# Gate and residual of the MLP moved to the third step from the end in every block, the gated sum by way of PSUM

## The chip, the cores and the metric

The kernel runs on one core of a Trainium2 chip. The core has a matrix engine (TensorE, "PE" in the profile), VectorE ("DVE"), ScalarE ("ACT"), GpSimd ("POOL"), and SyncE ("SP"), which here only issues the transfers. They run their own instruction queues in order and wait for each other by semaphores. The metric is the device time of one execution in microseconds (us), smaller is better.

## The reference, cut to what matters

One layer of a diffusion backbone over 2048 tokens of width 1024: attention and convolution, and then the MLP that the change is about. All in fp32.

```python
x_new = x + g1 * (concat([attn_x, conv_x]) @ w_out)
hx2 = modulate(rms_norm(x_new, norm2_g), sh2, sc2)
x_new = x_new + g2 * (square(relu(hx2 @ w_mlp1)) @ w_mlp2)   # w_mlp1 (1024, 4096), w_mlp2 (4096, 1024)
return rms_norm(x_new, final_g)
```

`g2` is the gate, one value for each of the 1024 columns; the first `x_new` on the last line but one is the residual.

## The kernel before

Every product is made of three matmuls on halves of the numbers (`mm3`, lines 89 to 92: high by high, high by low, low by high). So each weight that arrives from memory is split into a high part (a ScalarE copy) and a low part (a subtraction on VectorE or GpSimd).

The MLP (lines 1374 to 1540) goes over 4 blocks of 512 tokens (`NBL`; a block is `TB` = 4 tiles of 128 tokens) and in each block over 16 steps (`NC`), one for each 256 of the 4096 hidden columns. A step `(b, c)` has two halves:

- `hidden` makes the hidden columns of the block by a Strassen-like scheme: seven products named `11`, `s2`, `s1`, `12`, `s3`, `22`, `s4` into PSUM, with VectorE sums between them (lines 1459 to 1471). Line 1459 reads the product `s2`; the product `22` is written over it, so TensorE can't begin `22` before line 1459 is done.
- `second` multiplies the hidden columns by the rows of `w_mlp2`, one 128x1024 product for each of the 4 tiles, and VectorE adds it to the tile's running sum `ac` (line 1497; a copy at `c == 0`, line 1490). It is issued one step late, after `hidden` of the next step.

`load_w1` and `load_w2` fetch the weights of the coming step into four buffers (`raw`) and split them: line 1392 on ScalarE, 1393 on GpSimd, the sums `s1` to `s4` of the weights on VectorE (line 1398), and for `w_mlp2` lines 1422 and 1423.

The gate and the residual go in once for each block, at step `CX[b]`, line 1374:

```python
    CX = [NC - 1] * (NBL - 1) + [NC - 3]
```

There VectorE multiplies `ac` by `g2` (line 1501) and GpSimd adds the residual `xf` (line 1502), which is loaded into one of the two `tmp` buffers (line 1500). In blocks 0 to 2 this is the last step, 15; in block 3 it is step 13. For steps after `CX[b]`, the rows of `w_mlp2` are multiplied by `g2` before they are split, on GpSimd (line 1420): two such instructions a step, so four in block 3. After step 15 a tile is squared on ScalarE (line 1505, into the `xf` buffer where that is still held, else into PSUM), scaled (line 1507) and stored.

At a block's end the tokens of the next one are transposed: `trans_next` loads them (`xm`, line 1430, into the same two `tmp` buffers), TensorE transposes them (line 1255), and ScalarE, VectorE and GpSimd make the split tiles `X` of them (lines 1260 to 1273; GpSimd's part is line 1269, tile `xtl`). These are issued at a high priority. The order of the instructions on each engine, and the buffer that each tile gets, are set when the kernel is built, by a scheduler that goes by its own estimates.

PSUM is one tile, `pall`, used as four slots of 128x1024 in rotation: two for `hidden`, one for each 128x1024 product of `second`, one for each transposed tile.

Of the kernel before, what the change touches and what calls it, by code (L numbers as in the profile page):

```python
# [14 lines left out]
ALU = mybir.AluOpType  # L15
# [26 lines left out]
def hybrid_layer(ctx: ExitStack, tc: tile.TileContext, a: dict, out: bass.AP):  # L42
    nc = tc.nc
    TE, VE, SE, GE, SY = nc.tensor, nc.vector, nc.scalar, nc.gpsimd, nc.sync
# [9 lines left out]
    def psA(name, hold=None):  # L54
        i = free_ps.popleft()
        (free_ps if hold is None else hold).append(i)
        return pall[:, i * 1024:(i + 1) * 1024]
# [31 lines left out]
    def mm3(outp, lh, ll, rh, rl, start, stop):  # L89
        TE.matmul(outp, lh, rh, start=start, stop=False)  # L90
        TE.matmul(outp, lh, rl, start=False, stop=False)  # L91
        TE.matmul(outp, ll, rh, start=False, stop=stop)  # L92
# [35 lines left out]
    def rstd_of(dst, ss, n=D):  # L128
        SE.activation(dst, ss, AF.Sqrt, bias=epst[0:dst.shape[0]], scale=1.0 / n)
        VE.reciprocal(dst, dst)  # L130
# [1147 lines left out]
    def tmp(name):  # L1278
        return mp.tile([P, D], F32, tag="tmp", bufs=2, name=name)

    def row(name):
        return mp.tile([P, D], F32, tag="row", bufs=3, name=name)

    def acc(name):
        return mp.tile([P, D], F32, tag="ac", bufs=TB, name=name)
# [66 lines left out]
    g2, fg, pu = row("g2"), row("fg"), row("pu")  # L1352
# [21 lines left out]
    NC = FF // 256  # L1374
    NBL = S // (TB * P)

    CX = [NC - 1] * (NBL - 1) + [NC - 3]


    def load_w1(c, nm):  # L1380
# [32 lines left out]
    def load_w2(b, c, nm):  # L1413
        t = ttile(f"w2_{nm}", ring)
        ws = []
        for kh in range(2):
            r = raw(f"w2_{nm}{kh}r")
            SY.dma_start(r, w2[c * 256 + kh * P:c * 256 + (kh + 1) * P, :])
            if c > CX[b]:
                GE.tensor_tensor(r, r, g2, ALU.mult)  # L1420
# [56 lines left out]
    def second(b, c, hid, w2s):  # L1477
        for tt in range(TB):
            t = b * TB + tt
            o = tt * P  # L1480
            po_ = psA(f"pm{b}_{c}_{tt}")
            for n in range(2):
                for fc in range(2):
                    hh, hl = hid[0][:, fc, :], hid[1][:, fc, :]
                    wh, wl = w2s[fc]
                    mm3(po_[:, n * 512:(n + 1) * 512], hh[:, o:o + P], hl[:, o:o + P],
                        wh[:, n * 512:(n + 1) * 512], wl[:, n * 512:(n + 1) * 512], fc == 0, fc == 1)
            if c == 0:
                accs[tt] = acc(f"ac{b}{tt}")
                VE.tensor_copy(accs[tt], po_)  # L1490
                continue
            ac = accs[tt]
            xt = po_
            if b == NBL - 1 and c == NC - 1 and tt == TB - 1:
                last_tile(t, po_, ac)
                return
            VE.tensor_tensor(ac, po_, ac, ALU.add)  # L1497
            if c == CX[b]:
                xt = tmp(f"xf{t}")
                SY.dma_start(xt, xn_d[t * P:(t + 1) * P, :])  # L1500
                VE.tensor_tensor(ac, ac, g2, ALU.mult)  # L1501
                GE.tensor_tensor(ac, xt, ac, ALU.add)
            if c == NC - 1:
                ss = mp.tile([P, 1], F32, tag="ssf", bufs=2, name=f"ssf{t}")
                SE.activation(xt, ac, AF.Square, accum_out=ss)
                rstd_of(ss, ss)
                VE.scalar_tensor_tensor(ac, ac, ss, fg, ALU.mult, ALU.mult)
                SY.dma_start(out[t * P:(t + 1) * P, :], ac)


    def last_tile(t, po_, ac):
        ss = mp.tile([P, 2], F32, tag="ssl", bufs=1, name="ssl")
        hs = [slice(n * 512, (n + 1) * 512) for n in range(2)]
        for n, h in enumerate(hs):
            VE.tensor_tensor(ac[:, h], po_[:, h], ac[:, h], ALU.add)
            SE.activation(po_[:, h], ac[:, h], AF.Square, accum_out=ss[:, n:n + 1])
        VE.tensor_tensor(ss[:, 0:1], ss[:, 0:1], ss[:, 1:2], ALU.add)
        rstd_of(ss[:, 0:1], ss[:, 0:1])
        for h in hs:
            VE.scalar_tensor_tensor(ac[:, h], ac[:, h], ss[:, 0:1], fg[:, h], ALU.mult, ALU.mult)  # L1520
            SY.dma_start(out[t * P:(t + 1) * P, h], ac[:, h])
# [3 lines left out]
    for i, (b, c) in enumerate(steps):  # L1525
        if c == 0 and pend_ is not None:
            second(*pend_)
            pend_ = None
        w2s = load_w2(b, c, f"{b}_{c}")
        hid = hidden(f"{b}_{c}", w1n)  # L1530
        if b == 0 and 2 <= c < KD + 5:
            g2_step(c - 2)
        if i + 1 < len(steps):
            if c == 0 and b:
                with tc.issue_after(lv):
                    w1n = load_w1((c + 1) % NC, "%d_%d" % steps[i + 1])
            else:
                w1n = load_w1((c + 1) % NC, "%d_%d" % steps[i + 1])
        if c == NC - 1 and b + 1 < NBL:
            X = new_X(b + 1)  # L1540
            n0 = len(nc.cur_bb.bb.instructions)
            for tt in range(TB):
                with tc.high_priority(offset=3000):
                    trans_next(b + 1, tt)

            lv = last_of(VE, n0)
        if pend_ is not None:
            second(*pend_)
        pend_ = (b, c, hid, w2s)
    second(*pend_)  # L1550


# [56 lines left out]
```

## Time and profile before

| | |
|---|---|
| median of 3 runs | 2568.53 us (2560.25 to 2570.44) |
| profiled execution, its own time | 2570.69 us |
| its span | 2568.9 us |
| mean granted TensorE clock | 0.979 |
| busy share of the span: PE, DVE, ACT, POOL | 95%, 70%, 49%, 57% |
| a block of the MLP (from step 2 of block 1 to step 2 of block 2) | 354.6 us |

The span is what the engines' first and last instructions enclose; the kernel's time lies 1.8 us above it. Busy shares are means over the whole kernel, in which the MLP is the second half, from about 1160 us on. In a view of one engine in order of time, a row has its start, its length, the line, the operation, what it writes and reads, and, in square brackets, how long the engine sat idle ahead of it and what it waited for.

### The profile page before, as it was taken

The page shows a single profiled execution, that of the slowest core. Times are in us where ns is not written, and L with a number is a line of the kernel's source. Part 1 is how long each engine was busy: PE and PEld are TensorE (multiplying, and loading weights), DVE is VectorE, ACT ScalarE, POOL GpSimd, SP SyncE. Part 2 cuts the span into 40 slices and gives each one's busy share as a digit, 9 for nine tenths or more (in the row PEclk, how much of TensorE's full clock was granted, in tenths as well). Part 3 has the DMA queues.
Part 4 walks back from the last instruction along what each step waited for, and adds up shares of the span by engine and source line. Part 5 has one row for each costly group of instructions (what it writes and reads, how often), then busy time and mean ns, then how long its engine had stood idle before and what let it go on. Part 6 is the DMA issues. An engine that isn't in the chain of part 4 may idle for free.

```text
span 2568.9 us, 42313 instructions
## 1 busy us (share of the span) xinstructions
PE 2430.5 (95%) x15903; PEld 2216.9 (86%) x15903; DVE 1790.2 (70%) x2465; ACT 1248.7 (49%) x2162; POOL 1467.8 (57%) x1055
## 2 busy tenths in 40 slices
PE   7997989899889999988999999999999999999997
PEld 5985889689889999987998889999889998799996
DVE  6646743666689976468666697666786676876676
ACT  4334531443689963134444554444554445454442
POOL 3537422442578856457555676555675556755564
PEclk9998999999999999999999999999999999999999
DMA  8555764653899865665333443333343334433321
GB/s 299 158 168 163 223 216 130 196 154 110 227 253 262 241 182 174 195 231 165 99 99 107 129 139 111 101 105 99 121 148 101 99 99 126 137 107 100 105 92 57
DMA packets 293882, 387.26 MB, mean 151 GB/s; under 512 B 38021, under 2 KB 231228, under 8 KB 293644
## 3 DMA queue, kind: packets, MB, share of 16 engines
q1 hardware_dynamic: 293660, 384.54, 49.7%
q8 instruction: 125, 2.05, 0.3%
q14 instruction: 81, 0.66, 0.1%
q10 hardware_dynamic: 16, 0.00, 0.0%
HBM read 308.03 MB, written 86.76 MB: 154 GB/s over the span
## 4 chain that ended last, share of the span: by engine, by line
PE 62%; DVE 10%; DMA 9%; POOL 5%; issue 4%; SPq 2%; ACT 1%; DVEq 0%; POOLq 0%; ACTq 0%
PE pall L90 18%; PE pall L91 18%; PE pall L92 18%; PE pall L1105 2%; PE pall L1069 1%; PE pall L1030 1%; DVE s L1398 1%; DMA ar<-at_d 1%; DVE ac L1501 1%; DVE ac L1497 1%; PE pall L1107 1%; DVE w L1423 1%; PE pall L1032 1%; DMA cw<-h_d 1%; DMA xn_d<-xo 1%
## 5 line engine op out<-in xcount | busy, mean ns | idle before, releaser
L90 PE MATMUL pall<-w,hh 128*128 128x512 f32 x1024 | 406.0, 397 | 11.0 <-DVE ac L1497 7.2
L91 PE MATMUL pall<-w,hh 128*128 128x512 f32 x1024 | 403.0, 394 | 0.0
L92 PE MATMUL pall<-w,hl 128*128 128x512 f32 x1024 | 397.2, 392 | 0.6 <-DVE hl L1454 0.6
L1497 DVE TENSOR_TENSOR ac<-pall,ac 128x1024 f32<-128x1024 f32 x239 | 286.8, 1214 | 73.9 <-PE pall L92 73.2
L90 PEld LDWEIGHTS pall<-w,hh 128*128 128x128 f32 x1024 | 195.1, 190 | 51.6 <-issue 4.4
L92 PEld LDWEIGHTS pall<-w,hl 128*128 128x128 f32 x1024 | 193.3, 189 | 41.9 <-DVE hl L1454 2.2
L91 PEld LDWEIGHTS pall<-w,hh 128*128 128x128 f32 x1024 | 194.8, 190 | 36.4 <-issue 0.2
L1451 ACT ACTIVATE c<-c 128x512 f32<-128x512 f32 x128 | 80.9, 632 | 157.2 <-DVE c L1471 129.2
L86 POOL TENSOR_TENSOR w_0l<-w_0r,w_0h 128x1024 fp32r<-128x1024 f32 x20 | 50.7, 2537 | 172.7 <-ACT w_0h L85 152.5
L90 PE MATMUL pall<-xah,w 128*128 128x256 f32 x512 | 144.8, 284 | 4.7 <-ACT w L1392 4.7
L92 PE MATMUL pall<-xah,w 128*128 128x256 f32 x512 | 145.2, 284 | 0.0
L91 PE MATMUL pall<-xal,w 128*128 128x256 f32 x512 | 145.0, 283 | 0.0
L1454 DVE TENSOR_TENSOR hl<-c,hh 128x512 fp32r<-128x512 f32 x128 | 123.7, 967 | 15.3 <-ACT hh L1453 15.2
L1062 POOL TENSOR_SCALAR sb<-sb,ri 128x696 f32<-128x696 f32 (+1 forms) x128 | 105.6, 826 | 49.7 <-DVE ri L1057 40.7
L1044 DVE CUSTOM_DVE_ANT_0 sb<-pall,bias 128x696 f32<-128x696 f32 (+1 forms) x128 | 108.0, 845 | 6.5 <-PE pall L1032 5.9
L1052 ACT ACTIVATE sb<-sb,mn 128x696 f32<-128x696 f32 (+1 forms) x128 | 109.6, 857 | 0.6 <-DVE mn L1044 0.6
L90 PEld LDWEIGHTS pall<-xah,w 128*128 128x128 f32 x512 | 98.1, 192 | 7.5 <-ACT w L1392 4.9
L91 PEld LDWEIGHTS pall<-xal,w 128*128 128x128 f32 x512 | 98.6, 192 | 2.8
L92 PEld LDWEIGHTS pall<-xah,w 128*128 128x128 f32 x512 | 98.6, 192 | 2.1
L90 PE MATMUL pall<-xth,w 128*128 128x256 f32 x256 | 75.2, 294 | 19.1 <-DVE pu L1459 19.1
L1105 PE MATMUL pall<-pw,v 120*128 120x256 f32 (+1 forms) x480 | 90.8, 309 | 0.8 <-ACT ob L1112 0.8
L1081 DVE TENSOR_TENSOR pw<-pall,pw 120x512 fp32r<-120x512 f32 (+1 forms) x128 | 83.5, 653 | 5.1 <-ACT pw L1076 4.7
(853 smaller groups left out, 8797.0 us busy)
## 6 DMA issues: line engine op xcount, KB each, us to landing
v<-v_d SPq DMA_DIRECT2D x144, 120.0 KB
q<-q_d SPq DMA_DIRECT2D x64, 256.0 KB
wr<-in_w_ada SPq DMA_DIRECT2D x48, 256.0 KB
v_d<-vt SPq DMA_DIRECT2D x64, 160.0 KB
wa<-in_w_ada SPq DMA_DIRECT2D x8, 1024.0 KB
x<-in_x SPq DMA_DIRECT2D x16, 512.0 KB
kr<-k_d SPq DMA_DIRECT2D x32, 256.0 KB
at_d<-ao SPq DMA_DIRECT2D x32, 256.0 KB
```

What stands on the lines that cost most here:

```text
L86: (eng or GE).tensor_tensor(l, r, f(h), ALU.subtract)
L90: TE.matmul(outp, lh, rh, start=start, stop=False)
L91: TE.matmul(outp, lh, rl, start=False, stop=False)
L92: TE.matmul(outp, ll, rh, start=False, stop=stop)
L1044: VE.tensor_tensor_reduce(sb[:, c0:SE_], d["s"][:, 512 - SC0 + c0:768], bt[:, c0:SE_], -1.0, 3e38, ALU.add, ALU.min, mn)
L1052: SE.activation(pb[:, c0:SE_], pb[:, c0:SE_], AF.Exp, bias=d["mn"], scale=-1.0, accum_out=d["sm"])
L1062: GE.tensor_scalar(pb[:, c0:SE_], pb[:, c0:SE_], d["ri"], 1.0, ALU.mult, ALU.mult)
L1081: VE.tensor_tensor(pw[0:120, 0:nch, 1, :], d["tv"], f(pw)[0:120, 0:nch, 0, :], ALU.subtract)
L1105: TE.matmul(o, VT[(pr, *key)][0:n, hd, :], pw[0:n, ch, :, :], start=(ch == 0), stop=False)
L1451: SE.activation(c, c, AF.Relu)
L1454: VE.tensor_tensor(dl, cv, f(dh), ALU.subtract)
L1497: VE.tensor_tensor(ac, po_, ac, ALU.add)
```

## The change

`CX` becomes `[NC - 3] * NBL`: in every block the gate and the residual go in at step 13. In blocks 0 to 2 the rows of `w_mlp2` of steps 14 and 15 are therefore multiplied by `g2` on GpSimd (four more instructions of line 1420 a block, 12 in all). At the gated step, in all four blocks, the new product is added to the running sum in place in PSUM, and the multiplication reads PSUM and writes `ac`. At the last step the square goes into PSUM in all blocks, since `xf` isn't held any more.

```diff
-    CX = [NC - 1] * (NBL - 1) + [NC - 3]
+    CX = [NC - 3] * NBL
...
-            VE.tensor_tensor(ac, po_, ac, ALU.add)
             if c == CX[b]:
                 xt = tmp(f"xf{t}")
                 SY.dma_start(xt, xn_d[t * P:(t + 1) * P, :])
-                VE.tensor_tensor(ac, ac, g2, ALU.mult)
+
+                VE.tensor_tensor(po_, po_, ac, ALU.add)
+                VE.tensor_tensor(ac, po_, g2, ALU.mult)
                 GE.tensor_tensor(ac, xt, ac, ALU.add)
+                continue
+            VE.tensor_tensor(ac, po_, ac, ALU.add)
             if c == NC - 1:
```

In block 3 the order of all engines stays as it was; only the operands of the gate differ. In blocks 0 to 2 it changes from step 13 on. Three places follow, each at the end of block 0; blocks 1 and 2 have the same pattern. In the names, `ac00` to `ac03` are the block's four running sums, `_0_15` belongs to step 15 of block 0, and `_1_0` to step 0 of block 1.

VectorE, the end of step 14 in the kernel before: the last sums of step 13's products, the split of step 15's `w_mlp2`, and line 1459 of step 15's `hidden`, with a sum of the first transposed tile between them.

```order
L1497 TENSOR_TENSOR ac01_12650<-pall_66,ac01_12650 128x1024
L1454 TENSOR_TENSOR hl0_14_15083<-c0_14_15081,hh0_14_15082 128x2x4x64
L1497 TENSOR_TENSOR ac02_12664<-pall_66,ac02_12664 128x1024
L1497 TENSOR_TENSOR ac03_12678<-pall_66,ac03_12678 128x1024
L1423 TENSOR_TENSOR w2_0_15_15269<-w2_0_150r_15270,w2_0_15_15269 128x1024
L1261 TENSOR_TENSOR xs100_15430<-xs101_15431,pall_66 128x256
L1459 TENSOR_TENSOR pu_12299<-pall_66,pu_12299 128x256
```

The same place in the changed kernel, from the second tile's sum on.

```order
L1501 TENSOR_TENSOR pall_66<-pall_66,ac01_12650 128x1024
L1502 TENSOR_TENSOR ac01_12650<-pall_66,g2_12297 128x1024
L1454 TENSOR_TENSOR hl0_14_15085<-c0_14_15083,hh0_14_15084 128x2x4x64
L1398 TENSOR_TENSOR s1_1_0_15408<-w1_1_00r_15401,w1_1_01r_15403 128x512
L1501 TENSOR_TENSOR pall_66<-pall_66,ac02_12664 128x1024
L1398 TENSOR_TENSOR s2_1_0_15410<-s1_1_0_15408,w1_1_00r_15401 128x512
L1398 TENSOR_TENSOR s3_1_0_15421<-w1_1_00r_15401 128x512
L1502 TENSOR_TENSOR ac02_12664<-pall_66,g2_12297 128x1024
L1501 TENSOR_TENSOR pall_66<-pall_66,ac03_12678 128x1024
L1423 TENSOR_TENSOR w2_0_15_15287<-w2_0_150r_15288,w2_0_15_15287 128x1024
L1459 TENSOR_TENSOR pu_12299<-pall_66,pu_12299 128x256
L1502 TENSOR_TENSOR ac03_12678<-pall_66,g2_12297 128x1024
```

Ahead of line 1459 there now stand three of the four gate multiplications (the first is just above the rows shown) and the three weight sums of the next block's first step, which used to come earlier; the fourth multiplication follows it.

SyncE's queue of transfers, kernel before, the last step of block 0 and the start of block 1. Two `xm` tiles of the coming block (`xm10`, `xm11`) have been loaded much earlier, among the loads of step 3.

```order
L1418 DMA w2_1_00r_15665<-in_w_mlp2 128x1024
L1430 DMA xm12_15470<-xm_d_74 128x1024
L1418 DMA w2_1_01r_15669<-in_w_mlp2 128x1024
L1430 DMA xm13_15495<-xm_d_74 128x1024
L1384 DMA w1_1_10r_15776<-in_w_mlp1 128x4x256
L1384 DMA w1_1_11r_15778<-in_w_mlp1 128x4x256
L1500 DMA xf0_15585<-xn_d_73 128x1024
```

The same queue in the changed kernel. Here `xf0` and `xf1` are the ones that were loaded among the loads of step 3.

```order
L1384 DMA w1_1_01r_15403<-in_w_mlp1 128x4x256
L1499 DMA xf2_15265<-xn_d_73 128x1024
L1418 DMA w2_1_00r_15669<-in_w_mlp2 128x1024
L1499 DMA xf3_15282<-xn_d_73 128x1024
L1418 DMA w2_1_01r_15673<-in_w_mlp2 128x1024
L1384 DMA w1_1_10r_15780<-in_w_mlp1 128x4x256
L1430 DMA xm10_15440<-xm_d_74 128x1024
L1430 DMA xm11_15465<-xm_d_74 128x1024
L1430 DMA xm12_15490<-xm_d_74 128x1024
L1384 DMA w1_1_11r_15782<-in_w_mlp1 128x4x256
L1430 DMA xm13_15515<-xm_d_74 128x1024
```

With two `tmp` buffers, each of these tiles takes the buffer of the second one before it; all four `xm` now come after all four `xf`.

GpSimd in the changed kernel, the residual additions of block 0 (line 1503) and what stands between them.

```order
L1503 TENSOR_TENSOR ac00_12636<-xf0_15231,ac00_12636 128x1024
L1393 TENSOR_TENSOR w1_1_011_15405<-w1_1_00r_15401,w1_1_011_15405 128x512
L1503 TENSOR_TENSOR ac01_12650<-xf1_15248,ac01_12650 128x1024
L1423 TENSOR_TENSOR w2_0_15_15287<-w2_0_151r_15293,w2_0_15_15287 128x1024
L1503 TENSOR_TENSOR ac02_12664<-xf2_15265,ac02_12664 128x1024
L1393 TENSOR_TENSOR w1_1_0s2_15412<-s2_1_0_15410,w1_1_0s2_15412 128x512
L1393 TENSOR_TENSOR w1_1_0s1_15415<-s1_1_0_15408,w1_1_0s1_15415 128x512
L1393 TENSOR_TENSOR w1_1_012_15418<-w1_1_01r_15403,w1_1_012_15418 128x512
L1503 TENSOR_TENSOR ac03_12678<-xf3_15282,ac03_12678 128x1024
```

In the kernel before, these additions stood among the first splits of the next block, behind and between the eight of line 1269.

## Rows read from the trace of the kernel before

**Rows 1.** VectorE in order of time: line 1459, once a step (block 0).

```profile
1248.60 0.42 DVE L1459 TENSOR_TENSOR pu<-pall,pu 128x256 f32<-128x256 f32 x1 [0.47 <-ACT w_6s L1392]
1269.62 0.42 DVE L1459 TENSOR_TENSOR pu<-pall,pu 128x256 f32<-128x256 f32 x1 [0.47 <-ACT w_7s L1392]
```

**Rows 2.** Stretches: length, PE, PEld, DVE, ACT, POOL busy (instructions), clock, DMA, GB/s.

```profile
1600.00:1700.00 100.00, 100.00 (x638) 91.10 (x637) 67.73 (x85) 49.28 (x77) 60.65 (x40) 1.00 0.33 101
...
1522.00:1524.00 2.00, 2.00 (x10) 1.90 (x9) 1.90 (x2) 0.23 (x1) 1.83 (x2) 0.50 0.95 363
...
2533.00:2536.00 3.00, 1.08 (x5) 1.08 (x6) 2.90 (x5) 0.00 (x0) 1.84 (x2) 0.50 0.00 0
```

**Rows 3.** The forty 2-us stretches from 1464 to 1544 summed: first boundary.

```profile
sum 80.00, PE 71.06 PEld 63.21 DVE 70.05 ACT 44.34 POOL 64.31; mean PE 1.78 PEld 1.58 DVE 1.75 ACT 1.11 POOL 1.61
```

**Rows 4.** TensorE in order of time: two waits of the first boundary, all after 2450.

```profile
1474.04 0.66 PE L1255 MATMUL pall<-ident,xm 128*128 128x128 f32 x4 [2.04 <-DVE c L1471]
...
1520.63 0.58 PE L90 MATMUL pall<-xth,w 128*128 128x256 f32 x1 [2.20 <-DVE pu L1459]
...
2518.49 0.50 PE L90 MATMUL pall<-w,hh 128*128 128x512 f32 x1 [1.18 <-DVE c L1471]
2534.92 0.58 PE L90 MATMUL pall<-xth,w 128*128 128x256 f32 x1 [7.37 <-DVE pu L1459]
```

**Rows 5.** VectorE in order of time: the gate of block 3.

```profile
2511.29 1.77 DVE L1398 TENSOR_TENSOR s<-w_151r,s 128x512 f32<-128x512 f32 x1 [4.30 <-POOL w_15s L1393]
...
2515.79 2.31 DVE L1501 TENSOR_TENSOR ac<-ac,g 128x1024 f32<-128x1024 f32 x1
...
2519.60 1.99 DVE L1501 TENSOR_TENSOR ac<-ac,g 128x1024 f32<-128x1024 f32 x1
2521.51 2.89 DVE L1454 TENSOR_TENSOR hl<-c,hh 128x512 fp32r<-128x512 f32 x1
...
2525.57 2.18 DVE L1501 TENSOR_TENSOR ac<-ac,g 128x1024 f32<-128x1024 f32 x1
...
2528.81 2.45 DVE L1423 TENSOR_TENSOR w<-w_150r,w 128x1024 fp32r<-128x1024 f32 x1
2531.18 3.35 DVE L1501 TENSOR_TENSOR ac<-ac,g 128x1024 f32<-128x1024 f32 x1
2534.45 0.41 DVE L1459 TENSOR_TENSOR pu<-pall,pu 128x256 f32<-128x256 f32 x1
```

**Rows 6.** GpSimd in order of time: two transposed tiles of block 1, then block 3's gate.

```profile
1475.23 2.53 POOL L1269 TENSOR_TENSOR xtl<-xs,xth 128x512 fp32r<-128x512 f32 x2 [0.45 <-ACT xth L1268]
1480.87 2.55 POOL L1269 TENSOR_TENSOR xtl<-xs,xth 128x512 fp32r<-128x512 f32 x2 [3.11 <-ACT xth L1268]
...
2512.47 2.85 POOL L1420 TENSOR_TENSOR w_151r<-w_151r,g 128x1024 f32<-128x1024 f32 x1
...
2519.20 1.30 POOL L1393 TENSOR_TENSOR w_15s<-s,w_15s 128x512 fp32r<-128x512 f32 x1
...
2530.13 3.32 POOL L1423 TENSOR_TENSOR w<-w_151r,w 128x1024 fp32r<-128x1024 f32 x1
```

**Rows 7.** All sums into `ac`, gates, residual additions, squares into PSUM: shortest, median, longest ns.

```profile
L1497 DVE TENSOR_TENSOR ac<-pall,ac x239: 1199/1211/1226, 1193.0 to 2558.4; 128x1024 f32<-128x1024 f32 x120
...
L1501 DVE TENSOR_TENSOR ac<-ac,g x16: 1210/2164/3355, 1485.5 to 2531.2; 128x1024 f32<-128x1024 f32 x16
L1502 POOL TENSOR_TENSOR ac<-xf,ac x16: 2343/2602/3395, 1486.8 to 2534.6; 128x1024 f32<-128x1024 f32 x16
...
L1505 ACT ACTIVATE pall<-ac x3: 1029/1029/1030, 2554.2 to 2559.7; 128x1024 f32<-128x1024 f32 x3
```

**Rows 8.** A load of line 1384 as SyncE issues it, and VectorE's wait for it.

```profile
2493.72 0.38 SPq L1384 DMA_DIRECT2D w_151r<-in_w_mlp  x1
...
2497.53 0.69 DVE L1398 TENSOR_TENSOR s<-w_150r,w_151r 128x512 f32<-128x512 f32 x1 [3.53 <-DMA w_151r<-in_w_mlp]
```

## The prediction

> **What bounds the kernel now.** First the rhythm of a step: line 1459 comes once a step, and in the middle of a block two of them lie 21.02 us apart [rows 1]. In such a stretch TensorE is busy for all of 100 us at full clock, VectorE for 68 and GpSimd for 61 [rows 2]. A step has 84 matmuls of 256 columns and 48 of 512, or 180 units of 256 columns, so a unit takes 21.02 / 180 = 0.117 us. In mid-block nothing can be won but by fewer matmuls, and VectorE and GpSimd have a third to spare.
>
> Then the places where TensorE waits. At the first boundary it is idle for 80.00 - 71.06 = 8.94 us [rows 3]; the longest pieces are a transposition that waits for VectorE (2.04) and a product that waits for line 1459 (2.20) [rows 4]. After the last of these the granted clock is half (1.2 of 2.4 GHz) for some 3 us [rows 2], which costs about 1.4 us. So a boundary loses 8.9 + 1.4 = 10.3 us, three times over. Block 3 has no boundary, but its gate at step 13 makes TensorE wait 1.18 and 7.37 us, its only waits after 2450 us [rows 4], again with half clock behind it [rows 2]. This is the pattern that the change gives to all blocks, so block 3 is the best evidence for it.
>
> Last, why block 3 waits. The product `22` can't start until line 1459 is done, and VectorE comes to that line at 2534.45, 23.16 us after it began the weight sum at 2511.29 (itself held by GpSimd for 4.30) [rows 5]. The four gate multiplications in between take 2.31, 1.99, 2.18 and 3.35 us, while the shortest of all sixteen takes 1.21 [rows 5, 7]. The excess is waiting for GpSimd: the one of 3.35 us starts at 2531.18, in the middle of GpSimd's subtraction from 2530.13 to 2533.45, and ends 1.08 us after it [rows 5, 6]. The sums that read PSUM never show this: 239 of them lie between 1.199 and 1.226 us [rows 7].
>
> **Block 3: the multiplication reads PSUM.** The order of instructions there doesn't change. Four multiplications at 1.21 take 4.84 us where they took 9.83, so line 1459 comes 5.0 us earlier. The split of line 1454 (2.89) and of line 1423 (2.45) between them were held in the same way [rows 5]; alone they would take about 0.69 (a sum of 512 columns) [rows 8] and 1.21, so up to 3.4 us more can go, or none, since GpSimd has the same work to do. The gain is 5.0 to 8.4 of the 8.55 us of waits, and up to 1.4 of clock. The price of an addition that writes PSUM is not in the trace. The nearest rows are 1.21 for a sum from PSUM into SBUF and 1.03 for ScalarE's square that writes the same size into PSUM [rows 7]; I take 1.21, and as the bad bound 0.4 us more for each of four. That gives a gain of 3.4 to 9.8; I take **6.5**, nearer the rows of the multiplications alone. No slot is missed: the next products need this block's PSUM slots only after line 1459 anyway.
>
> The Trainium skill speaks against the route by PSUM (VectorE: DVE Perf Modes, the section on the TRN2 errata): it gives a fixed part of 120 cycles to a VectorE instruction that reads PSUM and 58 to one that reads SBUF. By it each multiplication would be some 0.065 us dearer (an estimate from those figures), and the sum 1 us worse over the sixteen. The rows of this case show no such difference, with 1.199 at the shortest from PSUM and 1.210 from SBUF.
>
> **Blocks 0 to 2: a gate at step 13.** From the same weight sum to line 1459, VectorE's row is block 3's with two differences: the fourth multiplication comes behind line 1459 (-1.21), and three weight sums of line 1398 stand in it. Alone these cost 0.69 each, 2.1 in all; if each waits for a residual addition (2.60) [rows 7] it is 9.9. I take 3.5, since only some will meet one. That makes 23.16 - 5.0 - 1.2 + 3.5 = 20.5 us, and 0.4 for line 1459 itself. TensorE was ready for `22` at 2534.92 - 7.37 = 2527.55, and 1.18 earlier without the first wait, so 15.1 us after the weight sum began. The wait is 20.9 - 15.1 = **5.8 us** (0.9 if the two splits get free as well and the sums stay at 2.1; 12.2 if all three meet an addition). Half clock behind it costs **1.4**, as in block 3.
>
> The four instructions of line 1420 take up to 2.85 us each on GpSimd [rows 6], 11.4 a block. In two steps GpSimd has 42 x 0.39 = 16 us free [rows 2], which hides them; without that cover they would hold the weights of the next step. I count **0.5** (0 to 2).
>
> The loads of the next block's tokens lose their head start. Before, two `xm` tiles lay ready in the `tmp` buffers; now these hold `xf`, and `xm11` gets its buffer only when GpSimd has done the fourth residual addition. Counted from the weight sum: the third multiplication ends at about 17.5 (a sum and line 1423 lie between it and line 1459), the third addition at 20.1, three splits of 1.30 [rows 6] make 24.0, the fourth addition 26.6, and a load took 3.8 us from issue to use (2493.72 to 2497.53) [rows 8], so 30.4. All later loads queue behind it on SyncE. TensorE has finished `22` and `s4` (24 units, 2.8 us, and 1.4 of clock) at 25.1 and the first transposition at 26.3. In its row the second transposition stands next, ahead of all of step 14's products, so it waits up to 4.1 us; I take **3.0** (0 to 6), as a load alone can land sooner.
>
> Each transposed tile then takes GpSimd, VectorE and ScalarE 5.64 us, one behind the other (1475.23 to 1480.87) [rows 6]. Four from 26.3 on end at 48.9. TensorE gets to the new block's first product after three transpositions and 60 matmuls of 512 columns (14.0 us), at about 48. I count **1.5** (0 to 5).
>
> What is taken from the boundary: four multiplications and the additions. VectorE was busy for 70 of the 80 us there, GpSimd for 64 [rows 3]; without them I leave **0.5** us (0 to 5) of TensorE's remaining waits, for VectorE no longer is late at line 1459 of step 1.
>
> **The sum.** A boundary with its gate: 5.8 + 1.4 + 0.5 + 3.0 + 1.5 + 0.5 = 12.7 us, against 10.3 before: +2.4, three times +7.2. Block 3: -6.5. Together +0.7 on the profiled execution's own 2570.69, so 2571.4. That execution lies 2.2 us above the median of the runs shown, so I predict **2569 us**.
>
> **The rivals.** *The transpositions come too late (slower).* The place is the queue of `xm` loads behind the residual additions. If the second transposition waits 5.5 and the first product of the new block 4, a boundary costs 17.7, or +7.4, and the time is 2569 + 15 = 2584. It decides from about 8.6 us for the two together (I took 4.5). For it speaks that all the links are in series and the row of TensorE is fixed; against it, that a boundary with VectorE less full may give some of it back later. Chance 0.22.
>
> *The gate hides (faster).* If VectorE's splits and sums hardly meet GpSimd, the gate's wait is 0.9 and the clock stays, so a boundary costs 6.4, or -3.9, and the time is 2568.5 - 11.7 - 6.5 = 2550. For it speaks that multiplications which don't meet GpSimd let its own queue run earlier; against it, the 4.30 us by which GpSimd already holds VectorE ahead of the gate [rows 5]. Chance 0.22.
>
> *The route by PSUM brings nothing.* If an addition into PSUM is as much dearer as the multiplication gets cheaper, block 3 gains nothing and each gate waits 5 us more: +7.4 a boundary, 2591. The flat 1.2 us of all sums from PSUM speak against it. Chance 0.06.
>
> **How the numbers follow.** The forecast keeps 0.50, with a range of its own of 2558 to 2580 (3 us more or less a boundary, 3 in block 3). The range of 2552 to 2585 takes in most of both rivals and leaves out the third. Within 0.5% of 2568.5, about what a measurement of this kernel can tell from no change, lie 2556 to 2581: same 0.50; faster, from the hidden gate, 0.22; slower, from the late transpositions and the dear route, 0.28.
>
> **What would show it.** In the profile after: gate multiplications all near 1.21 us; TensorE's wait for line 1459 in block 3 at 0 to 3.5 us in place of 7.37; at the end of blocks 0 to 2 a wait of about 6 us for line 1459 of step 15 with half clock behind it, then one of about 3 for `xm11` ahead of a transposition; few waits in steps 0 and 1. Wrong it would be if the gate's wait is under 2 or over 9, if an addition into PSUM is well over 1.21, or if the new block's first product waits over 4 us.

## The result: slower by 1.4%

The changed kernel takes 2603.91 us (median of 4 runs, 2599.93 to 2607.42); the kernel before, on the same chip, 2569.49. The ratio is 1.014, with a 95% interval of 1.0111 to 1.0169. The profiled execution took 2604.5 us with a span of 2602.6 and a mean granted clock of 0.967. I had forecast 2569, in a range up to 2585. One of the four runs of e9 below (2970.17 us, mean granted clock 0.749) fell into a slower state of the chip and is left out of its median and ratio.

TensorE's waits in the MLP of the changed kernel, grouped (total us, times, longest). In the kernel before, the same view has 19.1 us for line 1459, and no `xm` or `hh` row.

```profile
PE pall L90 <- DVE pu L1459: 31.8, 6, 8.3
PE pall L1255 <- DMA xm<-xm_d: 15.6, 6, 4.0
PE pall L90 <- ACT hh L1453: 13.1, 3, 5.2
PE pall L90 <- DVE ac L1505: 2.9, 4, 1.3
```

The same waits as TensorE meets them, in order of time, at the first boundary and in block 3 (these answer to [rows 4]).

```profile
1470.93 0.58 PE L90 MATMUL pall<-xth,w 128*128 128x256 f32 x1 [7.45 <-DVE pu L1459]
1477.57 1.97 PE L1255 MATMUL pall<-ident,xm 128*128 128x128 f32 x8 [2.20 <-DMA xm<-xm_d]
1483.58 3.67 PE L1255 MATMUL pall<-ident,xm 128*128 128x128 f32 x16 [4.04 <-DMA xm<-xm_d]
1491.58 0.47 PE L90 MATMUL pall<-w,hh 128*128 128x512 f32 x1 [0.53 <-DVE ac L1505]
...
1533.85 0.80 PE L90 MATMUL pall<-w,hh 128*128 128x512 f32 x1 [3.90 <-ACT hh L1453]
...
2555.20 0.50 PE L90 MATMUL pall<-w,hh 128*128 128x512 f32 x1 [0.97 <-DVE c L1471]
2568.34 0.39 PE L90 MATMUL pall<-xth,w 128*128 128x256 f32 x1 [4.04 <-DVE pu L1459]
```

Behind each of the three groups of waits at the boundary TensorE runs for most of a stretch at 1.2 of 2.4 GHz (granted clock 0.52 to 0.58 in the first three rows), where [rows 2] has one short stretch. Stretches of the changed kernel, with the columns of [rows 2]; the last row answers to [rows 3].

```profile
1470.00:1474.00 4.00, 3.07 (x14) 3.07 (x15) 3.53 (x8) 0.00 (x0) 4.00 (x3) 0.52 0.60 180
1476.00:1488.00 12.00, 6.39 (x28) 5.81 (x29) 8.06 (x13) 7.68 (x15) 10.25 (x8) 0.57 0.52 170
1532.00:1540.00 8.00, 6.15 (x17) 4.87 (x18) 5.39 (x7) 4.30 (x8) 6.49 (x5) 0.58 0.38 113
1460.00:1540.00 80.00, 61.87 (x355) 55.04 (x354) 64.96 (x84) 39.68 (x73) 58.12 (x34) 0.85 0.45 154
```

I added up, over stretches of 1 us around each boundary, the time in which TensorE was idle, and the busy time times (1 - granted clock), which is what half clock cost:

| idle + clock, us | boundary 0 | boundary 1 | boundary 2 | end of block 3 |
|---|---|---|---|---|
| before | 8.9 + 1.6 | 8.8 + 4.3 | 8.8 + 4.4 | 15.5 + 1.4 |
| changed | 18.1 + 6.8 | 17.5 + 6.7 | 20.4 + 7.2 | 12.2 + 1.7 |

The boundaries lose 40 us more (36.8 before, 76.7 now), block 3 loses 3 less. That makes +37; the spans differ by 33.7, and about 3 us less are spent outside these stretches.

VectorE in order of time, from the weight sum `s4` of step 15 to line 1459 of step 15, block 0 (this answers to [rows 5]).

```profile
1447.46 1.76 DVE L1398 TENSOR_TENSOR s<-w_151r,s 128x512 f32<-128x512 f32 x1 [3.07 <-POOL w_15s L1393]
1449.15 1.22 DVE L1501 TENSOR_TENSOR pall<-pall,ac 128x1024 f32<-128x1024 f32 x1
...
1454.68 1.22 DVE L1502 TENSOR_TENSOR ac<-pall,g 128x1024 f32<-128x1024 f32 x1
1455.83 2.79 DVE L1454 TENSOR_TENSOR hl<-c,hh 128x512 fp32r<-128x512 f32 x1
1458.54 1.78 DVE L1398 TENSOR_TENSOR s<-w_00r,w_01r 128x512 f32<-128x512 f32 x1
...
1461.38 1.76 DVE L1398 TENSOR_TENSOR s<-s,w_00r 128x512 f32<-128x512 f32 x1
1463.06 2.84 DVE L1398 TENSOR_TENSOR s<-w_00r 128x512 f32<-128x512 f32 x1
...
1468.09 2.45 DVE L1423 TENSOR_TENSOR w<-w_150r,w 128x1024 fp32r<-128x1024 f32 x1
1470.46 0.41 DVE L1459 TENSOR_TENSOR pu<-pall,pu 128x256 f32<-128x256 f32 x1
```

The chain takes 23.0 us, and the gate's own instructions in it are as short as forecast. All sixteen of each kind (shortest, median, longest ns; these answer to [rows 7]):

```profile
L1501 DVE TENSOR_TENSOR pall<-pall,ac x16: 1217/1218/1222, 1449.1 to 2562.5; 128x1024 f32<-128x1024 f32 x16
...
L1502 DVE TENSOR_TENSOR ac<-pall,g x16: 1206/1211/1226, 1452.0 to 2566.7; 128x1024 f32<-128x1024 f32 x16
```

What is late comes from GpSimd: the first row above waits 3.07 us for a split of line 1393. GpSimd in order of time, steps 13 to 15 of block 0 (these answer to [rows 6]).

```profile
1414.83 2.42 POOL L1420 TENSOR_TENSOR w_140r<-w_140r,g 128x1024 f32<-128x1024 f32 x1 [5.97 <-DMA w_140r<-in_w_mlp]
...
1440.16 2.41 POOL L1420 TENSOR_TENSOR w_150r<-w_150r,g 128x1024 f32<-128x1024 f32 x1 [7.53 <-DVE pu L1459]
1442.53 2.40 POOL L1423 TENSOR_TENSOR w<-w_141r,w 128x1024 fp32r<-128x1024 f32 x1
1444.89 2.54 POOL L1393 TENSOR_TENSOR w_15s<-s,w_15s 128x512 fp32r<-128x512 f32 x2
...
1448.63 2.87 POOL L1420 TENSOR_TENSOR w_151r<-w_151r,g 128x1024 f32<-128x1024 f32 x1
...
1455.67 2.40 POOL L1503 TENSOR_TENSOR ac<-xf,ac 128x1024 f32<-128x1024 f32 x1
```

GpSimd sits idle for 5.97 and 7.53 us in front of line 1420, because the row of `w_mlp2` isn't there yet (the second row names line 1459, which ended at that moment; its load was issued at 1436.50). Then it has 2.4 us of multiplication to do that it didn't have before (and 2.87 at 1448.63), and all splits stand in order behind it; from 1440 to 1465 it never rests. My 16 us of free GpSimd time were there, but ahead of the load, where nothing of line 1420 can go.

### The profile page after: what moved, and what is told of

Same layout as the page of the kernel before. It is cut to its first block, busy times and chain, and to the rows that moved or that the text cites. A ratio compares the mean times of both kernels' runs of the same rounds, so it can differ in the third digit from the quotient of the medians.

```text
span 2602.6 us, 42297 instructions
## 1 busy us (share of the span) xinstructions
PE 2442.3 (94%) x15903; PEld 2229.7 (86%) x15903; DVE 1791.3 (69%) x2465; ACT 1251.2 (48%) x2162; POOL 1490.2 (57%) x1067
## 4 chain that ended last, share of the span: by engine, by line
PE 61%; DMA 9%; DVE 8%; POOL 7%; issue 6%; SPq 1%; ACT 1%; DVEq 0%; POOLq 0%; ACTq 0%
PE pall L90 18%; PE pall L91 18%; PE pall L92 18%; POOL w L1393 1%; PE pall L1105 1%; DVE s L1398 1%; PE pall L1069 1%; DMA xm<-xm_d 1%; PE pall L1030 1%; DMA kr<-k_d 1%; DMA cw<-h_d 1%; DVE ac L1505 1%; DMA w_141r<-in_w_mlp 1%; POOL w_15s L1393 1%; PE pall L1255 1%
## 5 line engine op out<-in xcount | busy, mean ns | idle before, releaser
L90 PE MATMUL pall<-w,hh 128*128 128x512 f32 x1024 | 407.4, 398 | 19.0 <-ACT hh L1453 13.1
L1505 DVE TENSOR_TENSOR ac<-pall,ac 128x1024 f32<-128x1024 f32 x223 | 268.8, 1216 | 76.1 <-PE pall L92 75.4
L1454 DVE TENSOR_TENSOR hl<-c,hh 128x512 fp32r<-128x512 f32 x128 | 132.6, 1036 | 23.5 <-ACT hh L1453 23.1
L90 PE MATMUL pall<-xth,w 128*128 128x256 f32 x256 | 75.2, 294 | 31.8 <-DVE pu L1459 31.8
```

The lines of the kernel that those rows point to most:

```text
L1454: VE.tensor_tensor(dl, cv, f(dh), ALU.subtract)
```

## The experiments

All were timed against the kernel before on the same chip. Runs e1 to e4, e5 to e8, e9 to e12 and e13 to e16 were made on four different chips, where the kernel before took 2569.48, 2569.25, 2567.96 and 2566.76; so a difference between two medians of different groups carries up to 3 us of that. Diffs are against the changed kernel, if nothing else is said, and cut to the lines that matter.

| run | median us | ratio to before | 95% |
|---|---|---|---|
| e1_psum_alone | 2560.33 | 0.9963 | 0.9951 to 0.9974 |
| e2_move_alone | 2611.73 | 1.0169 | 1.0148 to 1.0190 |
| e3_xm_own_buffer | 2591.84 | 1.0089 | 1.0068 to 1.0111 |
| e4_no_residual_load | 2594.54 | 1.0096 | 1.0075 to 1.0116 |
| e5_no_w2_gate | 2571.57 | 1.0003 | 0.9994 to 1.0013 |
| e6_residual_narrow | 2577.09 | 1.0030 | 1.0017 to 1.0044 |
| e7_gate_narrow | 2591.16 | 1.0073 | 1.0051 to 1.0095 |
| e8_gate_step11 | 2595.08 | 1.0092 | 1.0072 to 1.0112 |
| e9_fifth_raw | 2586.65 | 1.0083 | 1.0058 to 1.0107 |
| e10_psum_alone_fifth_raw | 2567.04 | 0.9990 | 0.9973 to 1.0008 |
| e11_before_fifth_raw | 2571.35 | 1.0013 | 0.9999 to 1.0028 |
| e12_w2_gate_alone | 2576.63 | 1.0029 | 1.0014 to 1.0043 |
| e13_no_w2_gate_b012 | 2578.42 | 1.0041 | 1.0026 to 1.0056 |
| e14_no_w2_gate_xm_own | 2571.02 | 1.0018 | 1.0006 to 1.0029 |
| e15_w2_gate_on_vector | 2588.88 | 1.0081 | 1.0063 to 1.0099 |
| e16_psum_alone_w2_on_vector | 2554.78 | 0.9951 | 0.9936 to 0.9966 |

### The two halves of the change

**e1**, the route by PSUM alone, and **e2**, the move alone:

```diff
 e1
-    CX = [NC - 3] * NBL
+    CX = [NC - 1] * (NBL - 1) + [NC - 3]
...
-                continue
-            VE.tensor_tensor(ac, po_, ac, ALU.add)
+            else:
+                VE.tensor_tensor(ac, po_, ac, ALU.add)
 e2 (against the kernel before)
-    CX = [NC - 1] * (NBL - 1) + [NC - 3]
+    CX = [NC - 3] * NBL
```

> The gate stays where it was (step 15 in blocks 0 to 2, step 13 in block 3), and only the route by PSUM is taken. Theory (the place of the gate in blocks 0 to 2 costs the time): the sixteen multiplications take 1.22 us, block 3 gains the 3 us that it gained in the changed kernel, a boundary between blocks gains 0 to 3, and the time is 2555 to 2567. Rival (the additions that write PSUM are what costs, by holding a PSUM slot one instruction longer): the boundaries lose about 10 us each as in the changed kernel, and the time is 2590 to 2604.

> The gate goes in at step 13 in every block, but the sum and the multiplication stay in SBUF as in the kernel before. Theory (the place costs, the route helps): slower than the changed kernel by the 3 us that block 3 lost there, in each of four blocks, so 2610 to 2625, with TensorE waiting 10 to 13 us for line 1459 in each of blocks 0 to 2, where the changed kernel has 7.5 to 8.3. Rival (the route by PSUM costs): near the kernel before, 2565 to 2585.

The route makes the kernel faster, by 9 us; the move costs 42 by way of SBUF and 44 by way of PSUM (2603.91 - 2560.33). In e1 block 3 is 3.3 us shorter from line 1459 of step 12 to the end (106.7 for 110.0) and waits 4.18 us for the gate in place of 7.37; its three boundaries lose 28.8 us in place of 36.8. The rival of e1 is out. In e2 the wait for line 1459 is 9.1 us in each of blocks 0 to 2, a little less than the 10 to 13 expected.

### The late loads of xm

**e3** gives `xm` a buffer of its own; **e4** frees the `tmp` buffers by leaving out the residual's load.

```diff
 e3
-        xt = tmp(f"xm{b}{i}")
+        xt = mp.tile([P, D], F32, tag="xm", bufs=1, name=f"xm{b}{i}")
 e4
-                xt = tmp(f"xf{t}")
-                SY.dma_start(xt, xn_d[t * P:(t + 1) * P, :])
-                GE.tensor_tensor(ac, xt, ac, ALU.add)
+                GE.tensor_tensor(ac, g2, ac, ALU.add)
```

> The changed kernel, with a buffer of its own for the loads xm of the next block's tokens, so that they need not wait for the residual additions. Theory A (three causes in series: the gate's wait for line 1459, the late loads, and half clock behind each): the waits of the transpositions for xm, 15.6 us in all, and their half clock go, the waits for line 1459 (31.8 in the MLP) stay within 4 us, and the time is 2580 to 2592. Theory B (the late loads are the cause, and the waits of the later steps come from them): back to the kernel before or better, 2560 to 2575. Theory C (the loads only hide a wait behind them, for VectorE or GpSimd, which then shows in their place): 2598 to 2606.

> The changed kernel, but the residual is left out: GpSimd adds g2 in place of the loaded tile, so four additions stay and the two tmp buffers are free for the loads xm, two of which again come early. Theory A (gate wait, late loads and half clock add up): the transpositions' waits for xm go, the gate's wait for line 1459 of 7.5 to 8.3 a block stays, and the time is 2578 to 2592. Theory B (the loads are all of the cause): 2560 to 2575. Theory C (something else takes the place): 2598 to 2606.

Both win 9 to 12 us of 34, so theory B is out; e3 lies at the upper end of what theory A gave and e4 2.5 us above it. But the wait for line 1459 didn't stay, as theory A had it: the scheduler now puts the transposition ahead of that product, and there it waits nearly as long (5.8 to 6.9 us a boundary in both), for a PSUM slot that a gate multiplication (line 1502) still reads. In e3, TensorE at the first boundary:

```profile
1465.97 1.97 PE L1255 MATMUL pall<-ident,xm 128*128 128x128 f32 x8 [5.80 <-DVE ac L1502]
```

Whoever comes first in TensorE's row meets the late VectorE.

### What makes VectorE late

**e5** leaves out line 1420; **e6** and **e7** shorten one instruction and keep VectorE's row up to line 1459 of step 15, but for one pair of neighbours and the last multiplication in e7.

```diff
 e5
-            if c > CX[b]:
-                GE.tensor_tensor(r, r, g2, ALU.mult)
 e6
-                GE.tensor_tensor(ac, xt, ac, ALU.add)
+                GE.tensor_tensor(ac[:, :128], xt[:, :128], ac[:, :128], ALU.add)
 e7
-                VE.tensor_tensor(ac, po_, g2, ALU.mult)
+                VE.tensor_tensor(ac[:, :128], po_[:, :128], g2[:, :128], ALU.mult)
```

> The changed kernel without line 1420: the rows of w_mlp2 of steps 14 and 15 are not multiplied by g2 (this leaves that part of the gate out). Theory A (GpSimd's backlog ahead of the gate makes VectorE late): GpSimd has 11 us less a block ahead of line 1459 of step 15, its wait falls from 7.5 to 8.3 to under 5 a block, block 3's 4.0 too, and the time is 2575 to 2590. Theory B (VectorE's own row of sums, multiplications and splits makes it late): the waits stay within 1.5 us, and the time is 2595 to 2604.

> The changed kernel, with the residual added to the first 128 of 1024 columns only (the rest is left out); VectorE's row up to line 1459 of step 15 is the same. The four additions on GpSimd shrink from 2.6 to about 0.4 us. Theory A (GpSimd's backlog): the wait for line 1459 falls by 2 to 5 us a block, the loads xm come 4 to 6 us earlier, and the time is 2575 to 2588. Theory B (VectorE's own row): the wait for line 1459 stays within 1 us, only the xm waits (6.2, 4.8, 4.5 a boundary) shrink, and the time is 2588 to 2598.

> The changed kernel, with the gate's multiplication on the first 128 of 1024 columns only (the rest of the gate is left out); the sums into PSUM and the residual additions stay. Each of the four multiplications shrinks from 1.22 to about 0.25 us. Theory B (VectorE's own row): the wait for line 1459 falls by the 2.9 us of the three multiplications ahead of it, a block gains 3 to 6 us, and the time is 2586 to 2595. Theory A (GpSimd's backlog): VectorE is held in the same places for longer, the wait falls by less than 1.5, and the time is 2596 to 2604.

Line 1420 is worth 32 us, more than either theory gave it. The wait for line 1459 falls from 31.8 to 9.8 us in e5, to 16.8 in e6 and to 19.5 in e7. Shorter residual additions are worth 27 us, but only part of that is the gate's wait, for they also let `xm` come earlier (11.2 us of waits for 15.6). Shorter multiplications are worth 13. So both theories hold a part, and GpSimd's is much the larger. The 32 and the 27 don't add up: both take work from the same engine in the same steps.

**e8** moves the gate away from the block's end. In block 0 `g2` is finished only after step 12, so there it gates with an unfinished `g2`; its time stands for the place only.

```diff
-    CX = [NC - 3] * NBL
+    CX = [NC - 5] * NBL
```

> The changed kernel with the gate at step 11 in all four blocks, three steps further from the next block's loads, weight sums and transpositions; line 1420 then works in four steps a block. Theory D (what costs is that the gate meets the end of the block: the next block's weight sums and xm loads): the boundaries lose no more than in the kernel before, each gate makes TensorE wait at most the 5 us that block 3's did at step 13, and the time is 2545 to 2572. Theory E (a gate costs 8 us of waits wherever it stands, and line 1420 slows each step that has it by 1 us): 2585 to 2605.

Theory D fails. In block 1 line 1459 comes 22.4, 21.4, 30.8 and 19.5 us after the one before it in the steps with line 1420 and the gate, where undisturbed steps take 21.0: 10 us lost far from any transposition. The time is in theory E's range.

### Line 1420 alone, with the gate, and without the late loads

**e12** adds line 1420 to e1, where the gate stays at step 15; **e13** takes it out of blocks 0 to 2 of the changed kernel; **e14** is e13 with the buffer of e3.

```diff
 e12 (against e1)
-            if c > CX[b]:
+            if c > NC - 3:
 e13
-            if c > CX[b]:
+            if c > CX[b] and b == NBL - 1:
```

> The first experiment (gate at step 15 by PSUM), with line 1420 in steps 14 and 15 of all blocks as in the changed kernel (so the rows of w_mlp2 of these steps are gated twice in blocks 0 to 2, which changes the result); the move of the gate is left out. Theory F: line 1420 alone slows the loads, each block of 0 to 2 gets 3 to 9 us longer, 2570 to 2588. Theory G, or that only both together are too much: under 2566.

> The changed kernel, with line 1420 left out in blocks 0 to 2 only (so the rows of w_mlp2 of their steps 14 and 15 are not gated); block 3 keeps it. It closes a square with the first experiment (gate late, no line 1420 in blocks 0 to 2), the one with line 1420 alone and the changed kernel. If GpSimd's multiplications and the gate hinder each other, line 1420 costs more here than the 16 us that it costs alone: 2575 to 2582, that is 22 to 29 us under the changed kernel. If the two costs only add up: 2586 to 2590.

> As the run before it, and with a buffer of its own for the loads xm. If line 1420 and the late loads xm are all that the move costs, this is back at the first experiment: 2558 to 2566. If the gate's own eight VectorE instructions a block still cost something at step 13 (the transposition that waits for a PSUM slot held by the gate): 2567 to 2578.

| | without line 1420 in blocks 0 to 2 | with it |
|---|---|---|
| gate at step 15 | 2560.3 (e1) | 2576.6 (e12) |
| gate at step 13 | 2578.4 (e13) | 2603.9 (the change) |

By these medians line 1420 costs 16 us alone and 25.5 beside the gate, and the move without it 18. The sum would be 2594.7, so 9 us would come from the two meeting. With each run set against the kernel before of its own chip, the costs are 18, 23 and 21, and 5 us are left for the meeting, which the spread of the runs doesn't tell from nothing. Without line 1420 the wait for line 1459 at the first boundary is 1.92 us, not 7.45. The rows of VectorE in e13, from line 1459 of step 14 to line 1459 of step 15, tell why.

```profile
1439.89 0.42 DVE L1459 TENSOR_TENSOR pu<-pall,pu 128x256 f32<-128x256 f32 x1 [0.47 <-ACT w_15s L1392]
...
1444.48 1.52 DVE L1398 TENSOR_TENSOR s<-w_151r,s 128x512 f32<-128x512 f32 x1
...
1466.57 0.41 DVE L1459 TENSOR_TENSOR pu<-pall,pu 128x256 f32<-128x256 f32 x1
```

The chain from the weight sum on is hardly shorter, 22.1 us for 23.0. But it begins 4.6 us after the line 1459 ahead of it, where the changed kernel needs 7.7 (1439.75 to 1447.46), since the sum doesn't wait for a split of GpSimd. The order of VectorE's row changes too without line 1420 (the three weight sums of the next block stand further up, and all four multiplications ahead of line 1459), so e5, e13 and e14 test line 1420 together with that order; e6 keeps the order.

In e12, where no gate is near, VectorE shows both ways in which line 1420 reaches it: the split that it waits for is late, and the load behind it.

```profile
1444.81 1.77 DVE L1398 TENSOR_TENSOR s<-w_151r,s 128x512 f32<-128x512 f32 x1 [3.06 <-POOL w_15s L1393]
...
1455.66 0.69 DVE L1398 TENSOR_TENSOR s<-w_00r,w_01r 128x512 f32<-128x512 f32 x1 [3.20 <-DMA w_01r<-in_w_mlp]
```

The first of these waits isn't there in e1, and the second is 2.00. SyncE issues the two loads in front of it 9.55 us apart in e12 (the first two rows below) and 6.72 in e1 (the two after them), since the buffer of the second one is freed by a split on GpSimd that stands behind line 1420 and ends at 1451.83 in e12 (the last fence).

```profile
1442.30 0.38 SPq L1384 DMA_DIRECT2D w_00r<-in_w_mlp  x1
1451.85 0.38 SPq L1384 DMA_DIRECT2D w_01r<-in_w_mlp  x1
```

```profile
1443.26 0.38 SPq L1384 DMA_DIRECT2D w_00r<-in_w_mlp  x1
1449.98 0.38 SPq L1384 DMA_DIRECT2D w_01r<-in_w_mlp  x1
```

```profile
1450.53 1.30 POOL L1393 TENSOR_TENSOR w<-w_151r,w 128x512 fp32r<-128x512 f32 x1
```

The buffer for `xm` (e14) gives 7 us back. Then 11 us over e1 stay (13 with each set against the kernel before of its chip), spread over waits of TensorE of 0.5 to 5.2 us each around the boundary and in the steps after it.

### Buffers or GpSimd's row

**e9** to **e11** give the weights a fifth `raw` buffer, in the changed kernel, in e1 and in the kernel before; `load_w1` gets the same edit as `load_w2`.

```diff
+    nraw = [0]
...
+    def raw5(name):
+        nraw[0] += 1
+        if nraw[0] % 5 == 0:
+            return mp.tile([P, 1024], F32, tag="R5", bufs=1, name=name)
+        return raw(name)
...
-            r = raw(f"w2_{nm}{kh}r")
+            r = raw5(f"w2_{nm}{kh}r")
```

> The changed kernel with five raw buffers for the weights in place of four. Theory F (line 1420 holds each raw buffer of w_mlp2 some 2.5 us longer, the four buffers turn in 24 us a step in place of 21, and all loads, splits and sums of steps 14, 15 and of the next block's step 0 come late): with a fifth buffer the loads come ahead of their use, the waits for line 1459 (31.8 us in the MLP) fall to under 15, and the time is 2565 to 2585. Theory G (it is the sheer work of GpSimd, the 12 multiplications and 12 additions that come earlier): the waits stay within 5 us and the time is 2595 to 2605.

> The gate at its old place by the route of PSUM (the first experiment), with five raw buffers. Theory F: only block 3 has line 1420 there, and its wait of 4 us for line 1459 goes with it; the boundaries win 0 to 3 each, since loads come earlier there too: 2545 to 2558. Theory G: no difference that can be measured from the first experiment, 2557 to 2563.

> The kernel before with five raw buffers, as the base for the fifth buffer. Theory F: block 3's gate wins some 2 to 6 of its 8.5 us of waits, the boundaries little: 2555 to 2566. Theory G: 2566 to 2572. If it gains as much as the changed kernel gains from the fifth buffer, the buffer is good for something else than line 1420.

The fifth buffer gives the changed kernel 15 us by the ratios. The waits for line 1459 fall from 31.8 to 10.8 us, as theory F had it, but the time stays above its range. Elsewhere the buffer brings nothing, and e1 even loses 7, which neither theory had; so it is good for line 1420, but not for all of it. GpSimd's row in e9 fits that (line 1428 there is line 1420): the first multiplication hardly waits any more, but the second does.

```profile
1435.12 2.40 POOL L1428 TENSOR_TENSOR w_150r<-w_150r,g 128x1024 f32<-128x1024 f32 x1 [0.58 <-DMA w_150r<-in_w_mlp]
1442.02 3.45 POOL L1428 TENSOR_TENSOR w_151r<-w_151r,g 128x1024 f32<-128x1024 f32 x1 [4.50 <-DMA w_151r<-in_w_mlp]
```

**e15** and **e16** do line 1420 on VectorE, in the changed kernel and in e1.

```diff
-                GE.tensor_tensor(r, r, g2, ALU.mult)
+                VE.tensor_tensor(r, r, g2, ALU.mult)
```

> The changed kernel, with the multiplications of line 1420 on VectorE in place of GpSimd. Theory F' (GpSimd stands idle for 6 to 7.5 us until the rows of w_mlp2 arrive, and then has 5 us more to do with all later splits queued behind it): VectorE needs 1.2 to 2.2 us for what takes GpSimd 2.4 to 2.9, GpSimd's row is as without line 1420, and the time is 2576 to 2592. Theory H (VectorE is the late engine at the gate, so more work on it costs more): 2605 to 2625.

> The first experiment (gate at step 15 by PSUM in blocks 0 to 2), with the four multiplications of line 1420 in block 3 on VectorE. Theory F': block 3's wait of 4 us for line 1459 shrinks, 2553 to 2559. Theory H: block 3 gets longer, 2562 to 2570.

Both are faster, by 15 and 5.5 us (12 and 3 with each set against the kernel before of its chip), so theory H is out. In e16 block 3 takes 101.9 us from line 1459 of step 12 to the end, against 106.7 in e1, and TensorE's wait for the gate is gone; the whole-run intervals of e1 and e16 still overlap, so the gain is shown for block 3 and not for the whole run. Line 1420 of e16 (shortest, median, longest ns):

```profile
L1420 DVE TENSOR_TENSOR w_140r<-w_140r,g x1: 1225/1225/1225, 2468.4 to 2468.4; 128x1024 f32<-128x1024 f32 x1
...
L1420 DVE TENSOR_TENSOR w_151r<-w_151r,g x1: 2350/2350/2350, 2498.5 to 2498.5; 128x1024 f32<-128x1024 f32 x1
```

e16, with the gate at step 15 in blocks 0 to 2, the route by PSUM, and line 1420 on VectorE, has the lowest median of all: 2554.78 us.

## Why the prediction was wrong

**The step that failed** is the one on line 1420: "In two steps GpSimd has 42 x 0.39 = 16 us free", which was to hide it, with 0.5 us counted. Measured, leaving it out of blocks 0 to 2 gives 25.5 us back, 8.5 a boundary (e13), and e13's 2578.42 lies inside my range. Two things were wrong in the step. The free time was a share of a mean, and it lies ahead of the load that line 1420 waits for, not behind it. And the four residual additions, which I moved into the same two steps, take another 9.6 us of GpSimd (four of 2.39, their median in the changed kernel); I didn't set them against the cover at all. Shortening them alone gives 27 us back over all blocks (e6; part of it by way of `xm`), so line 1420 isn't alone in keeping GpSimd late.

The terms of the sum, in us over the three boundaries, show where the loss came out. The last column is e13, added up in the same way.

| | forecast | the change | without line 1420 (e13) |
|---|---|---|---|
| the gate's wait for line 1459 | 17.4 | 24.0 | 6.5 |
| half clock | 4.2 | 20.7 | 12.4 |
| the transpositions' waits for `xm` | 9.0 | 15.6 | 14.5 |
| the first product of the new block | 4.5 | 0 | 0 |
| TensorE's remaining waits | 1.5 | 16.4 | 15.2 |
| line 1420 | 1.5 | in the rows above | none |
| sum | 38.1 | 76.7 | 48.6 |

So two more terms were mis-sized by themselves, also without line 1420: half clock and the remaining waits. That e13 comes out inside my range is in part luck, as its short wait for the gate makes up for these two.

**The gate's wait for line 1459**, forecast 5.8, is 7.45, 8.26 and 8.26 us. Without line 1420 it is 1.92, 2.30 and 2.29, so most of what line 1420 costs comes out in this term. I came near it only because I had worked it out from block 3, whose rows already have line 1420 in them. In it, the three weight sums of line 1398 took 6.4 us (1.78, 1.76, 2.84), where I took 3.5, and the two splits stayed as long as in block 3.

**Half clock**, forecast 1.4 once a boundary, costs 6.8, 6.7 and 7.2 us, since it comes behind each group of waits and not only behind the gate. The transpositions run in it too: 3.67 us for the sixteen at 1483.58, where in e14 eight take 1.09. And the base of 10.3 a boundary was that of the first; the other two lost 13.1 and 13.2 before.

**The transpositions**, forecast 3.0, wait 6.2, 4.8 and 4.5 us. The mechanism is as forecast (all `xm` behind all `xf`, and SyncE's queue held for 8.87 us by three of them).

```profile
1471.50 8.87 SPq L1430 DMA_DIRECT2D xm<-xm_d  x3
```

The rival of the late transpositions was right in its place but not in its second half, the new block's first product; by e3's 12 us and e14's 7 us it is the smaller part of the loss. The new block's first product (1.5) doesn't wait at any boundary. The remaining waits (0.5) did come: 3.9, 3.9 and 5.2 us for ScalarE's `hh` in step 1, as ScalarE stood in order behind a split of weights that waited 3.88 us for a VectorE sum (read from the rows of the first boundary; no run tests it).

**Block 3**, forecast -6.5, gives -3.2 to -3.3 (the change 106.8, e1 106.7, before 110.0). The multiplications shrank as forecast, and the chain with them, from 23.16 to 18.77 us; but VectorE began the chain later, 5.19 us of waiting for a split of GpSimd in place of 4.30, lines 1454 and 1423 took 2.77 and 3.14, and half clock came behind the gate as before (1.7 us). Without line 1420 (e5) the same stretch takes 99.7.

**The gate's multiplication** and the price of a sum into PSUM (1.21 forecast, 1.22 measured) were right; the rival that the route brings nothing is refuted by e1. The rival that the gate hides is out as well.

The Trainium skill's rule on shared ports (SBUF — State Buffer, section "Who interferes with whom") says that a VectorE instruction with both inputs in SBUF contends with a GpSimd instruction that reads SBUF, and one with at most one SBUF input doesn't. The rows agree: the split of line 1454, both inputs in SBUF, takes 2.79 us beside a GpSimd addition and 0.67 to 0.69 in the 58 places where GpSimd is idle beside it, while the sixteen multiplications with one input in PSUM stay within 1.206 to 1.226, though thirteen of them have GpSimd's splits or additions beside them. In the kernel before, the six multiplications from SBUF with GpSimd idle beside them take 1.210 to 1.216, and the ten with GpSimd busy 1.985 to 3.355.

**What stays open.** Line 1420 delays splits, and through them the loads, since GpSimd's splits free the buffers; how much each of the two costs isn't settled, for the fifth buffer changes the order on all engines as well, and leaving line 1420 out changes VectorE's. Of the 11 us that e14 keeps over e1, no single cause was tested.

## What to carry to other kernels

Idle time of an in-order engine covers new work only if it lies behind the data that this work waits for: look at what the engine was waiting for when it was idle, and where the new instruction stands in its row, before a mean busy share is used as cover. Work of several edits that lands in the same steps is charged against that cover together. When a change has two parts, time each alone: here one part gained 9 us and the other lost 44. A term that is taken from rows of another place brings along what else stands in these rows: block 3's gate had line 1420 in it.

## What was not expected of the hardware

A sum that reads and writes the same PSUM tile takes 1.217 to 1.222 us for 128x1024, no more than a sum from PSUM into SBUF (1.199 to 1.226 in [rows 7]). The fixed part of 120 cycles for PSUM against 58 for SBUF, which the Trainium skill gives (VectorE: DVE Perf Modes, the section on the TRN2 errata), would make the multiplication from PSUM some 0.065 us dearer (an estimate from that page); its median here, 1.211, is that of the shortest ones from SBUF (1.210). The same section also says that its 58 falls short, and that an fp32 addition of two tensors takes (N + 151) / 0.96 ns, or 1.224 us for 1024 columns (an estimate from that page); the 1.210 lies within 0.02 us of this formula, where the 58 would give 1.127 (an estimate too), so the prediction had taken the wrong one of the two.

The sum of TensorE's idle time doesn't tell what the clock will cost. At the first boundary of e14 TensorE is idle for 11.2 us, more than in the kernel before (8.9), nearly all of it in eight waits of 0.70 to 1.72 us, and the granted clock stays at 2.4 GHz throughout; in the kernel before, the longest wait is 2.20 us and half clock costs 1.6. The first boundary of e14 as one stretch:

```profile
1460.00:1540.00 80.00, 68.81 (x430) 60.45 (x429) 65.76 (x90) 43.44 (x81) 59.21 (x36) 1.00 0.47 152
```
